# Eighteen of 24 gate tiles moved behind the first feed-forward stage, by seven products, and kept in HBM

## The chip, the cores and the metric

The kernel runs on one core of one Trainium2 chip. The metric is the device time of one execution in microseconds (us), shown as the median of the runs. One execution was also recorded by the hardware profiler; its span runs from the first to the last instruction.

## The reference, cut to what matters

Two layers of an encoder are applied to 656 tokens at once: 16 meta tokens and 512 prompt tokens (positions 0 to 527), and 8 streams of 16 sample tokens. Each layer is a feed-forward stage, a mixer and a second feed-forward stage. The gate logits that this change is about are 3 x 1024 of the 5376 columns of one projection; they scale the three branches of the mixer.

```python
h = x + 0.5 * swiglu(rmsnorm(x, n1), f1g, f1u, f1d)
u = rmsnorm(h, nm)
proj = u @ w_in
a_in, xb, gb, gc, q, k, v, g_logits = jnp.split(proj, cuts, axis=-1)
...
g = jax.nn.sigmoid(g_logits).reshape(bsz, t, N_BRANCH, D_MODEL)
mixed = g[:, :, 0] * y_a + g[:, :, 1] * y_b + g[:, :, 2] * y_c
h = h + mixed @ w_out
h = h + 0.5 * swiglu(rmsnorm(h, n2), f2g, f2u, f2d)
```

The inner sizes are D_MODEL 1024 and D_FF 2816, all in float32.

## The kernel before

Tokens lie along the free dimension and features along the 128 partitions, so the state `H` is 8 tiles of 128 x 656. Every float32 factor is split into a high and a low part (`split`: ScalarE (ACT) copies, VectorE (DVE) subtracts), and a product takes three matmuls (`mm3`, L145). A weight column tile of 1024 x 128 is loaded by SP into a `raw` buffer and split into two "slabs" (`prep_next`).

The work is one list of units, in order: first feed-forward stage, mixer, second feed-forward stage, for each of two layers (`build`, L1306). `run_units` takes them one after the other, and `pump` loads and splits the weights of the units that follow. A planner at build time then orders the instructions of each engine by simulated times, so neighbouring units interleave on TensorE (PE).

**A plain unit** (`unit`, `run_halves`, `col_unit`) is one column tile: 8 row tiles x 3 matmuls x 2 halves of the tokens = 48 matmuls. **A pair unit** (`pair_unit`, `run_pair`, L707) makes two column tiles by a seven-product scheme: x is kept as four blocks (two halves of the rows by two halves of the tokens) and four sums of them, and the seven products of 4 row tiles each take 7 x 4 x 3 = 84 matmuls of 328 columns where two plain units take 96. Its results come out over PSUM copies (ACT) and additions (DVE), and its weight sums are made by DVE or by accumulating DMAs that POOL issues (`grow`, L416). The feed-forward stages are made of pair units except for the first two column tiles of each matrix; the mixer is made of plain units alone.

**What feeds a stage.** The last units of a stage (`hu_down`) add to `H` and call `feed` (L526). For a feed-forward stage this writes the blocks of x with the old scale `rstd` in them and their four sums (`blocks`, `combine`), and the products are multiplied by `factor` = new scale x `root` of the old one. For the mixer it writes x times the gain alone, half by half (`gained`), and the products are multiplied by `rstd`. The new scale needs a sum over all 8 tiles and a chain of ACT and DVE steps (`scales`, `scale_of`).

**The mixer** (`mixer_units`, L1154) is 20 units for keys, queries, values, pool and conv, then 6 units for the gate tiles j = 0 and 1 (three branches each); attention jobs run beside them. After `done_gates` come 8 y units (`hu_y`, L1141), each with the three gate units of tile j + 2 behind it while there are any; then 8 w_out units. A y unit multiplies three PSUM results by the three gates, adds them and splits the sum, for each half of the tokens. In the second layer the gates and the y units leave the meta tokens out: their halves have 320 columns, not 328 (`EQ_OUT`). Gate tiles of even j lie in `gate[0]`, of odd j in `gate1`.

**Buffers.** The feed-forward stages have 8 slabs and 4 raw buffers, the mixer 4 and 2. PSUM has 2 banks named mm, 4 named z and 2 named aux. SP issues the weight loads in order; POOL issues the accumulating DMAs.

Of the kernel before, what the change touches and what calls it, by code (L numbers as in the profile page):

```python
# [10 lines left out]
P = 128  # L11
# [45 lines left out]
class Builder:  # L57
    def __init__(self, nc, tc, pools, t):
        self.nc, self.tc, self.t = nc, tc, t
        self.sb, self.wp, self.rp, self.pp = pools  # L60
# [95 lines left out]
    def setup(self):  # L156
# [17 lines left out]
        self.X = self.XR[:, 0:10496].rearrange("p (s k c) -> p s k c", s=2, k=KD)  # L174
        self.Pm = self.XR[:, 10496:15744].rearrange("p (s k c) -> p s k c", s=2, k=4)
        self.O = self.XR[:, 15744:20992].rearrange("p (s k c) -> p s k c", s=2, k=4)
# [8 lines left out]
        self.gate = [W[:, 0:1968], None]  # L185
# [340 lines left out]
    def feed(self, to, l, m, hi):  # L526

        c0, c1 = self.halves[hi]
        gain = {"mixer": "mix_norm", "ffn1": "ffn1_norm", "ffn2": "ffn2_norm"}[to]
        if to == "mixer":  # L530
            self.gained(self.H[:, m, c0:c1], l, m, c0, c1, gain)
        if hi == 0:
            return
        c0 = self.halves[0][0]
        n = c1 - c0
        if to != "mixer":
            self.blocks(l, m, gain, c0, n // 2)
        acc, s = self.acc[:, :n], self.sq[self.fed % 2][:, :n]
        if self.fed == 0:
            self.act(acc, self.H[:, m, c0:c1], AF.Square)  # L540
        else:
            self.act(s, self.H[:, m, c0:c1], AF.Square)
            if self.fed == KD - 1:
                self.tt(acc, acc, s, ALU.add)
            else:
                self.grow(acc, s)
        self.fed += 1
        if self.fed == KD:
            self.fed = 0
            halves = self.halves  # L550
            self.pending = lambda: self.scales(to, halves)
# [33 lines left out]
    def gained(self, h, l, m, c0, c1, gain):  # L585

        g = self.col(gain, l, m)
        hi, lo = (self.X[:, s, m, c0:c1] for s in range(2))
        return (self.act(hi, h, AF.Identity, scale=g),
                self.stt(lo, h, g, hi.bitcast(F32), ALU.mult, ALU.subtract))  # L590

    def scales(self, to, halves):

        at = halves[0][0]
        for c0, c1 in halves:
            n = c1 - c0
            ps = self.psum("aux")[:, :n]
            self.mm(ps, self.ones, self.acc[:, c0 - at:c1 - at], True, True)
            self.scale_of(ps, c0, c1, to != "mixer", self.na_f, self.nb_f)
# [41 lines left out]
    def col_unit(self, w, f, r, run):  # L641

        return dict(slabs=[4, 4], src=[(KD, [(0, KD, w[:, (f + r) * P:(f + r + 1) * P])])], prep=self.prep_plain,
                    run=self.run_col, evict=run, ring="F", r=r, i=0)
# [24 lines left out]
    def half_col(self, u, hi):  # L669
# [4 lines left out]
        S = self.sil if u["evict"] == self.gate_out else self.up  # L674
# [32 lines left out]
    def run_pair(self, u):  # L707
# [6 lines left out]
        S = self.sil if u["evict"] == self.gate_out else self.up  # L714
        S = S[:, :4 * n]
# [36 lines left out]

    def seven(self, u, bank, q, n, start):
# [19 lines left out]
    def x_at(self, s, k, c0, c1):  # L773
        return self.X[:, s, k, c0:c1]
# [35 lines left out]
    def scaled(self, out, ps, c0, c1):  # L810
        self.mul(out, ps, self.rstd[:, c0:c1])
# [25 lines left out]
    def hu_a(self, u, hi):  # L837
# [11 lines left out]
        else:  # L849
            n = TP - c0  # L850
            self.scaled(xp[:, PSTATE + c0:], ps[:, :n], c0, TP)
            self.mul(xs[:, :, PSTATE:], self.sample(ps[:, n:]), self.sample(self.rstd[:, TP:T]))
# [85 lines left out]
    def hu_gc(self, u, hi):  # L938
# [7 lines left out]
        else:  # L946
# [5 lines left out]
            self.mul(o, self.sample(ps[:, n:]), self.sample(self.rstd[:, TP:T]))  # L952
# [161 lines left out]

    def gate_unit(self, l, j, c):
        return self.w_in_unit(l, COL_G + 8 * c + j, self.hu_gate_logit, j=j, c=c)

    def hu_gate_logit(self, u, hi):
        ps, c0, c1 = self.w_in_product(u, hi)
        g = self.gate_of(u["j"])[:, 656 * u["c"] + c0:656 * u["c"] + c1]  # L1120
        self.scaled(g, ps, c0, c1)
        if u["j"] > 1:
            self.act(g, g, AF.Sigmoid)

    def gate_of(self, j):
        return self.gate1 if j % 2 else self.gate[0]
# [14 lines left out]
    def hu_y(self, u, hi):  # L1141
# [12 lines left out]
    def mixer_units(self, l):  # L1154
# [19 lines left out]
        def done_gates():  # L1174
# [131 lines left out]
    def build(self):  # L1306
# [23 lines left out]
        self.flush()  # L1330

# [231 lines left out]
def build_kernel(nc, tc, t):  # L1563
    from contextlib import ExitStack
    with ExitStack() as es:
# [5 lines left out]
        Builder(nc, tc, (sb, wp, rp, pp), t).build()  # L1571
# [42 lines left out]
```

## Time and profile before

| | |
|---|---|
| device time, median of 3 runs | 2848.79 us (2844.69 to 2854.1) |
| the profiled execution: device time | 2850.67 us |
| the profiled execution: span | 2849.0 us |
| PE busy | 2818.7 us, 99% |
| DVE busy | 1864.9 us, 65% |
| ACT busy | 1320.9 us, 46% |
| matmuls | 19179 |
| mean granted TensorE clock | 0.996 |

The time outside the span is 1.67 us. An engine's busy share is over the whole span; stages differ, so the rows below are taken by stage. A row of the timeline ends with the idle time of its engine before it and what ended that, in brackets.

### The profile page before, as it was taken

How to read it: one execution, taken by the hardware profiler on the slowest of the kernel's cores; microseconds unless marked ns; L12 is line 12 of the kernel's file. 1: busy time of each engine (PE TensorE's matmuls, PEld its weight loads, DVE VectorE, ACT ScalarE, POOL GpSimd, SP SyncE). 2: the span in 40 equal slices, each digit the busy share in tenths (PEclk: the TensorE clock that was granted, in tenths of full speed). 3: DMA queues.
4: the chain of work that ended last, by engine and by line, in shares of the span. 5: the costliest groups of instructions: out<-in, count | busy, mean ns of one | idle time of the engine just before them, and what ended most of it. 6: DMA issues, size and time to landing. Idle time of an engine off the chain costs nothing.

```text
span 2849.0 us, 48187 instructions
## 1 busy us (share of the span) xinstructions
PE 2818.7 (99%) x19179; PEld 2778.8 (98%) x19179; DVE 1864.9 (65%) x3442; ACT 1320.9 (46%) x2540; POOL 208.3 (7%) x305
## 2 busy tenths in 40 slices
PE   7999999999999999999999999999999999999999
PEld 6999999999999999999999999999999999999999
DVE  7675665876454776575786665768764457675764
ACT  5353444776332444353553443557763234443443
POOL 0001000011000001000000010001110000000010
PEclk8999999999999999999999999999999999999999
DMA  3545444222222345454435454442222224444452
GB/s 111 129 122 124 119 111 104 78 79 71 60 75 75 94 109 137 108 128 115 115 91 133 122 127 103 111 104 81 71 68 67 77 78 120 108 122 117 126 124 73
DMA packets 500244, 290.96 MB, mean 102 GB/s; under 512 B 14046, under 2 KB 477090, under 8 KB 500018
## 3 DMA queue, kind: packets, MB, share of 16 engines
q1 hardware_dynamic: 474468, 239.78, 29.2%
q0 software_dynamic: 25056, 47.79, 9.7%
q8 instruction: 150, 2.46, 0.4%
q14 instruction: 76, 0.62, 0.1%
q10 hardware_dynamic: 494, 0.32, 0.0%
HBM read 231.74 MB, written 8.31 MB: 84 GB/s over the span
## 4 chain that ended last, share of the span: by engine, by line
PE 94%; DVE 4%; DMA 2%; ACT 0%; issue 0%; SPq 0%; ACTq 0%; DVEq 0%
PE z L143 57%; PE mm L143 35%; DVE Wa L131 1%; PE aux L143 1%; DVE XR L134 1%; DVE ws L134 0%; DVE Wa L134 0%; DMA raw<-in_ffn_w_up_dram 0%; DMA raw<-in_ffn_w_gate_dram 0%; DVE slabs L134 0%; DMA xtok<-in_x_prompt_dram 0%; PE aux L1097 0%; PE z L1257 0%; DMA rawb<-rawb 0%; PE aux L1077 0%
## 5 line engine op out<-in xcount | busy, mean ns | idle before, releaser
L143 PE MATMUL mm<-XR,ws 128*128 128x328 f32 (+3 forms) x4848 | 799.3, 314 | 1.8 <-DVE Wa L134 1.8
L143 PEld LDWEIGHTS mm<-XR,ws 128*128 128x128 f32 x4848 | 737.1, 188 | 6.3 <-issue 2.9
L143 PE MATMUL z<-XR,ws 128*128 128x328 f32 (+3 forms) x3924 | 629.7, 312 | 10.0 <-ACT XR L120 5.9
L143 PEld LDWEIGHTS z<-XR,ws 128*128 128x128 f32 x3924 | 596.3, 189 | 11.6 <-ACT XR L120 6.4
L143 PE MATMUL z<-ra,ws 128*128 128x328 f32 (+1 forms) x2688 | 421.0, 311 | 0.8 <-DVE H L131 0.8
L120 ACT ACTIVATE ws<-raw 128x512 fp32r<-128x512 f32 (+1 forms) x429 | 264.3, 618 | 332.9 <-PE z L143 203.9
L143 PEld LDWEIGHTS z<-ra,ws 128*128 128x128 f32 x2688 | 405.1, 188 | 1.1 <-DVE H L131 1.0
L134 DVE TENSOR_TENSOR ws<-raw,ws 128x512 fp32r<-128x512 f32 (+1 forms) x429 | 288.1, 673 | 179.6 <-ACT ws L120 178.3
L143 PE MATMUL z<-ra,slabs 128*128 128x328 f32 (+1 forms) x2112 | 330.0, 312 | 0.0
L143 PEld LDWEIGHTS z<-ra,slabs 128*128 128x128 f32 x2112 | 319.2, 188 | 0.1
L143 PE MATMUL mm<-XR,slabs 128*128 128x328 f32 (+1 forms) x1944 | 316.7, 312 | 1.0 <-ACT Wa L120 1.0
L143 PE MATMUL z<-XR,slabs 128*128 128x328 f32 (+1 forms) x1764 | 296.5, 314 | 4.7 <-DVE Wa L134 4.7
L143 PEld LDWEIGHTS mm<-XR,slabs 128*128 128x128 f32 x1944 | 296.4, 188 | 1.4 <-ACT Wa L120 1.3
L143 PEld LDWEIGHTS z<-XR,slabs 128*128 128x128 f32 x1764 | 273.5, 190 | 5.4 <-DVE Wa L134 5.3
L134 DVE TENSOR_TENSOR Wa<-Wa 128x328 f32<-128x328 f32 (+5 forms) x325 | 215.5, 668 | 34.5 <-ACT Wa L120 31.0
L131 DVE SCALAR_TENSOR_TENSOR H<-z,H 128x328 f32<-128x328 f32 (+1 forms) x288 | 140.9, 493 | 141.2 <-PE z L143 140.8
L120 ACT ACTIVATE Wa<-Wa 128x656 f32<-128x656 f32 (+7 forms) x232 | 136.9, 597 | 98.1 <-DVE Wa L134 94.1
L120 ACT ACTIVATE slabs<-raw 128x512 fp32r<-128x512 f32 (+1 forms) x183 | 109.4, 601 | 156.6 <-PE z L143 75.3
L120 ACT ACTIVATE ws<-rawb 128x512 fp32r<-128x512 f32 (+1 forms) x183 | 109.5, 601 | 148.7 <-PE z L143 91.3
L120 ACT ACTIVATE slabs<-rawb 128x512 fp32r<-128x512 f32 (+1 forms) x181 | 107.4, 599 | 141.8 <-PE z L143 101.0
L120 ACT ACTIVATE Wa<-mm 128x328 f32<-128x328 f32 (+1 forms) x240 | 105.4, 439 | 141.2 <-PE mm L143 140.3
L134 DVE TENSOR_TENSOR ws<-rawb,ws 128x512 fp32r<-128x512 f32 (+1 forms) x183 | 118.8, 653 | 61.8 <-ACT ws L120 60.8
(181 smaller groups left out, 2549.8 us busy)
## 6 DMA issues: line engine op xcount, KB each, us to landing
raw<-in_w_in_dram SPq DMA_DIRECT2D x88, 512.0 KB, 3.7
raw<-in_ffn_w_gate_dram SPq DMA_DIRECT2D x57, 512.0 KB, 3.7
rawb<-in_ffn_w_up_dram SPq DMA_DIRECT2D x55, 512.0 KB, 4.9
rawb<-in_ffn_w_down_dram SPq DMA_DIRECT2D x48, 384.0 KB, 3.4
raw<-in_ffn_w_down_dram SPq DMA_DIRECT2D x48, 384.0 KB, 3.4
raw<-in_ffn_w_up_dram SPq DMA_DIRECT2D x33, 512.0 KB, 4.4
rawb<-in_ffn_w_gate_dram SPq DMA_DIRECT2D x31, 512.0 KB, 3.6
Wa<-in_ffn_w_gate_dram SPq DMA_DIRECT2D x36, 256.0 KB
```

The lines of the kernel that those rows point to most:

```text
L120: i = self.nc.scalar.activation(out, in_, func, **kw).ins
L131: return self.nc.vector.scalar_tensor_tensor(out, in0, scalar, in1, op0=op0, op1=op1).ins
L134: self.nc.vector.tensor_tensor(out, in0, in1, op=op)
L143: self.nc.tensor.matmul(out, lhsT, rhs, start=start, stop=stop, skip_group_check=True)
```

## The change

For each layer, the 18 gate tiles j = 2 to 7 leave the mixer. They are computed right behind the first feed-forward stage: two as plain column units, sixteen as eight pair units, over all 656 tokens in both layers. Each result goes through the sigmoid on ACT, and ACT's DMA queue stores it (128 x 656) to a tile in HBM. In the y stage POOL's DMA queue reads the three tiles of a j back into one of four places (`gates[0..2]` and `gate1`): j = 2 and 3 after `done_gates`, j + 4 after y unit j. The mixer reads x from the four blocks that `feed` now always writes, so its products are scaled by `factor`, of which `enter` keeps a copy in `root`; `done_y` puts `root` back as 1/`rstd`. `Pm` and `O` take the place of the four sums. The y units but the last add and split both halves at once.

```diff
-        if to == "mixer":
-            self.gained(self.H[:, m, c0:c1], l, m, c0, c1, gain)
         if hi == 0:
             return
...
-        if to != "mixer":
-            self.blocks(l, m, gain, c0, n // 2)
+        self.blocks(l, m, gain, c0, n // 2)
...
     def scaled(self, out, ps, c0, c1):
-        self.mul(out, ps, self.rstd[:, c0:c1])
+        self.mul(out, ps, self.root[:, c0:c1])
...
+    def early_gates(self, l):
+        w = self.t["w_in"][l]
+        units = []
+        for j in range(2, KD, 2):
+            for c in range(3):
+                f = COL_G + 8 * c + j
+                if not units:
+                    units = [self.col_unit(w, f, r, self.early_gate, j=j, c=c) for r in range(2)]
+                else:
+                    units.append(self.pair_unit(w, f, self.early_gate, soon=len(units) == 2, j=j, c=c))
+        return units
+
+    def early_gate(self, u, r, n):
+        s = self.place(u)[:, 2 * n * r:2 * n * (r + 1)]
+        self.act(s, s, AF.Sigmoid)
+        self.nc.scalar.dma_start(self.kept[3 * (u["j"] + r - 2) + u["c"]], s)
+
+    def load_gate(self, j):
+        if j < KD:
+            at = 3 * (j - 2)
+            self.nc.gpsimd.dma_start(self.gate_of(j).rearrange("p (c t) -> p c t", c=3),
+                                     self.kept[at:at + 3].rearrange("c p t -> p c t"))
...
     def gate_of(self, j):
-        return self.gate1 if j % 2 else self.gate[0]
+        return (self.gates[0], self.gate1, self.gates[1], self.gates[2])[j % 4]
...
             self.mul(g[c], self.product(ps, u["w"], x, ks, xks, c0, c1), g[c])
+        if j < KD - 1:
+            if hi == 0:
+                return
+            c0 = self.halves[0][0]
+            g = [self.gate_of(j)[:, 656 * c + c0:656 * c + c1] for c in range(3)]
         self.tt(g[0], g[0], g[1], ALU.add)
...
+            for j in range(2, 4):
+                self.load_gate(j)
         U[-1]["after_it"] = done_gates
         for j in range(KD):
             U.append(self.y_unit(l, j))
-            if j + 2 < KD:
-                for c in range(3):
-                    U.append(self.gate_unit(l, j + 2, c))
+            U[-1]["after_it"] = lambda j=j: self.load_gate(j + 4)
         self.last_y = len(U) - 1
-        U[-1]["after_it"] = self.ffn_columns
+
+        def done_y():
+            self.ffn_columns()
+            self.nc.vector.reciprocal(self.root, self.rstd)
+        U[-1]["after_it"] = done_y
...
             units += self.ffn_units(l, 1, ("mixer", l))
+            g = self.early_gates(l)
+            g[0]["before"] = lambda l=l: self.new_gates(l)
+            units += g
 
             def enter(l=l):
+                self.late()
+                self.nc.vector.tensor_copy(self.root, self.factor)
```

`place` gives column units and every second pair unit the buffer `sil`, the others `up`.

## Rows read from the trace of the kernel before

**Rows 1.** The page's first part: busy time, share of the span, instructions.
```profile
PE 2818.7 (99%) x19179; PEld 2778.8 (98%) x19179; DVE 1864.9 (65%) x3442; ACT 1320.9 (46%) x2540; POOL 208.3 (7%) x305
```

**Rows 2.** Stretches: length, each engine's busy time (instructions), clock, DMA share, GB/s.
```profile
20.00:100.00 80.00, 69.53 (x440) 67.78 (x441) 71.97 (x144) 47.15 (x95) 1.87 (x2) 0.94 0.30 83
...
372.00:426.00 54.00, 54.00 (x362) 54.00 (x361) 42.14 (x71) 29.31 (x56) 4.61 (x6) 1.00 0.48 121
...
745.00:938.00 193.00, 193.00 (x1285) 193.00 (x1284) 96.19 (x182) 58.38 (x108) 0.00 (x0) 1.00 0.26 74
938.00:997.00 59.00, 59.00 (x395) 59.00 (x394) 42.55 (x67) 24.98 (x36) 5.24 (x6) 1.00 0.42 95
...
1443.00:1458.00 15.00, 15.00 (x99) 14.65 (x98) 14.56 (x25) 8.32 (x12) 0.00 (x0) 1.00 0.20 52
```

**Rows 3.** The chain that ended last, in order of time: start, us, what.
```profile
737.83 7.22 PE z L143 x48
...
2173.87 7.04 PE z L143 x48
```

**Rows 4.** PE's timeline: its waits of over 1 us from 100 us on.
```profile
1016.89 9.02 PE L143 MATMUL z<-XR,slabs 128*128 128x328 f32 x48 [1.87 <-DVE Wa L134]
...
1908.69 0.55 PE L1077 MATMUL aux<-ident,Wa 128*128 128x128 f32 x3 [1.07 <-DVE Wa L131]
...
1911.00 3.78 PE L143 MATMUL mm<-XR,ws 128*128 128x384 f32 x20 [1.77 <-DVE Wa L134]
...
2409.60 0.85 PE L143 MATMUL z<-XR,ws 128*128 128x320 f32 x4 [1.13 <-ACT XR L120]
2423.66 8.84 PE L143 MATMUL z<-XR,slabs 128*128 128x320 f32 x48 [2.87 <-DVE Wa L134]
```

**Rows 5.** Groups by line and shape: busy us, mean ns; then idle time before.
```profile
L134 DVE TENSOR_TENSOR ws<-raw,ws 128x512 fp32r<-128x512 f32 x405 | 278.3, 688 | 177.1 <-ACT ws L120 175.8
...
L120 ACT ACTIVATE ws<-raw 128x512 fp32r<-128x512 f32 x405 | 254.4, 629 | 317.3 <-PE z L143 195.4 <-PE mm L143 84.2 <-issue 8.7
...
L134 DVE TENSOR_TENSOR Wa<-Wa 128x656 f32<-128x656 f32 x130 | 108.8, 837 | 1.5
...
L120 ACT ACTIVATE Wa<-mm 128x328 f32<-128x328 f32 x180 | 79.2, 440 | 103.1 <-PE mm L143 102.4
L134 DVE TENSOR_TENSOR Wa<-z,Wa 128x328 f32<-128x328 f32 x160 | 78.8, 494 | 52.1 <-PE z L143 48.1 <-ACT Wa L120 1.8
...
L120 ACT ACTIVATE Wa<-Wa 128x656 f32<-128x656 f32 x66 | 49.2, 748 | 32.8 <-DVE Wa L134 29.8 <-DVE Wa L131 2.6
...
L418 POOL DMA_DIRECT2D raw<-raw x36 | 31.0, 862 | 119.0 <-DVE Wa L131 33.3 <-DVE H L131 20.7 <-DVE ws L134 19.4
...
L112 ACT ACT_TABLE_LOAD x12 | 15.4, 1283 | 1.0 <-PEq L1602 0.8
```

**Rows 6.** DMA: queues (packets, MB, share of 16 engines), then issues (KB, us to landing).
```profile
q1 hardware_dynamic: 474468, 239.78, 29.2%
q0 software_dynamic: 25056, 47.79, 9.7%
...
raw<-in_w_in_dram SPq DMA_DIRECT2D x88, 512.0 KB, 3.7
...
Wa<-Wa POOLq DMA_DIRECT2D x24, 328.0 KB, 4.1
...
raw<-in_pool_proj_dram SPq DMA_DIRECT2D x16, 128.0 KB, 2.2
```

**Rows 7.** Timeline, first layer: the last attention output, y unit 0, an issue on SP.
```profile
734.05 0.44 PE L143 MATMUL z<-val 128*64 128x128 f32 x4
...
753.01 1.07 PE L143 MATMUL mm<-XR,ws 128*128 128x328 f32 x6
...
760.97 0.37 SPq L333 DMA_DIRECT2D raw<-in_pool_proj_dram  x1
```

More of the change, by code (lines that the diff above doesn't have):

```diff
@@ L59, in __init__ @@
         self.nc, self.tc, self.t = nc, tc, t
-        self.sb, self.wp, self.rp, self.pp = pools
+        self.sb, self.wp, self.rp, self.pp, self.dp = pools
         self.halves = HALF_ALL
@@ L173, in setup @@
         self.XR = sb.tile([P, XR], F32R, tag="XR", name="XR")
-        self.X = self.XR[:, 0:10496].rearrange("p (s k c) -> p s k c", s=2, k=KD)
-        self.Pm = self.XR[:, 10496:15744].rearrange("p (s k c) -> p s k c", s=2, k=4)
-        self.O = self.XR[:, 15744:20992].rearrange("p (s k c) -> p s k c", s=2, k=4)
+        v = self.XR.rearrange("p (s k e c) -> p s k e c", s=2, k=4, e=4)
+        self.X = [v[:, :, :, e, :] for e in range(2)]
+        self.Pm, self.O = v[:, :, :, 2, :], v[:, :, :, 3, :]
         scale = sb.tile([P, 2 * T], F32, tag="scale", name="scale")
@@ L184, in setup @@
         self.nb = W[:, o + 4 * 384:o + 5 * 384]
-        self.gate = [W[:, 0:1968], None]
+        self.gates = [W[:, 1968 * i:1968 * (i + 1)] for i in range(3)]
         o += 1968
@@ L550, in feed @@
             halves = self.halves
-            self.pending = lambda: self.scales(to, halves)
+            self.pending = lambda: self.scales(halves)
     def part(self, j):
@@ L583, in xs, with scales @@
         return self.XR[:, o:o + blocks * n]
[L585 to L592, printed above, removed]
+    def scales(self, halves):
         at = halves[0][0]
@@ L598, in scales @@
             self.mm(ps, self.ones, self.acc[:, c0 - at:c1 - at], True, True)
-            self.scale_of(ps, c0, c1, to != "mixer", self.na_f, self.nb_f)
+            self.scale_of(ps, c0, c1, True, self.na_f, self.nb_f)
     def scale_of(self, ps, c0, c1, factor, a, b):
@@ L639, in pair_unit, with col_unit @@
                     a21=w[0:4 * P, c[1]].rearrange("(k p) c -> p k c", p=P), **kw)
-    def col_unit(self, w, f, r, run):
+    def col_unit(self, w, f, r, run, **kw):
         return dict(slabs=[4, 4], src=[(KD, [(0, KD, w[:, (f + r) * P:(f + r + 1) * P])])], prep=self.prep_plain,
-                    run=self.run_col, evict=run, ring="F", r=r, i=0)
+                    run=self.run_col, evict=run, ring="F", r=r, i=0, **kw)
     def run_col(self, u):
@@ L673, in half_col @@
         ps = self.product(self.psum("z"), u["w"], x, SLOTS, SLOTS, c0, c1)
-        S = self.sil if u["evict"] == self.gate_out else self.up
+        S = self.place(u)
         self.mul(S[:, (2 * r + hi) * n:(2 * r + hi + 1) * n], ps, self.factor[:, c0:c1])
@@ L713, in run_pair @@
         f = self.factor[:, c0:c0 + 2 * n]
-        S = self.sil if u["evict"] == self.gate_out else self.up
-        S = S[:, :4 * n]
+        S = self.place(u)[:, :4 * n]
         s = [S[:, i * n:(i + 1) * n] for i in range(4)]
@@ L751, in run_pair, with place @@
         self.slot_tail()
+    def place(self, u):
+        if u["evict"] == self.early_gate:
+            return self.up if u.get("turn") else self.sil
+        return self.up if u["evict"] == self.up_out else self.sil
     def seven(self, u, bank, q, n, start):
@@ L773, in x_at @@
     def x_at(self, s, k, c0, c1):
-        return self.X[:, s, k, c0:c1]
+        return self.X[k // 4][:, s, k % 4, c0:c1]
     def pm_at(self, s, k, c0, c1):
@@ L851, in hu_a @@
             self.scaled(xp[:, PSTATE + c0:], ps[:, :n], c0, TP)
[L852 removed]
+            self.mul(xs[:, :, PSTATE:], self.sample(ps[:, n:]), self.sample(self.root[:, TP:T]))
             assert self.history
@@ L951, in hu_gc @@
             o = xs[:, :, 2:]
-            self.mul(o, self.sample(ps[:, n:]), self.sample(self.rstd[:, TP:T]))
+            self.mul(o, self.sample(ps[:, n:]), self.sample(self.root[:, TP:T]))
             self.mul(o, o, self.sample(self.cB[:, TP:T]))
@@ L1330, in build, with new_gates @@
         self.flush()
+    def new_gates(self, l):
+        self.kept = self.dp.tile([3 * (KD - 2), P, T], F32, tag=f"gates{l}", name=f"gates{l}")
     def load_consts(self):
@@ L1570, in build_kernel @@
               for tag, n in (("mm", 2), ("z", 4), ("aux", 2))}
-        Builder(nc, tc, (sb, wp, rp, pp), t).build()
+        dp = es.enter_context(tc.tile_pool(name="dram", bufs=1, space=bass.MemoryType.DRAM))
+        Builder(nc, tc, (sb, wp, rp, pp, dp), t).build()
 _INS = ["x_prompt", "x_sample", "cache_k", "cache_v", "state_pool", "state_conv", "meta", "ffn1_norm",
```

5 lines of the change are left out of this document (1 added, 4 removed).

## The prediction, made before the changed kernel was run

> **What bounds the kernel now.** I read the busy shares first: PE is at work for 2818.7 of 2849.0 us [rows 1]. So the time is the number of matmuls times what one takes, plus about 30 us in which PE stands; a change pays by matmuls it drops, and costs where it makes PE stand. Second, the stretches: in the y stage, from 745 to 938 us, PE works 193.00 of 193.00 us, with DVE at 96.19 and ACT at 58.38 [rows 2]. Nothing there but the matmul count can be shortened. Third, the chain: 48 matmuls of 328 columns take 7.22 us, 48 of 320 columns 7.04 us [rows 3], so 150.4 and 146.7 ns each. Last, PE's waits: behind the first 100 us five exceed 1 us, all at the opening of a stage, 8.7 us together [rows 4].
>
> **1. The matmuls.** Before, a layer's 18 gate tiles take 18 x 48 = 864 matmuls. After, two column units take 96 and eight pair units 8 x 84 = 672, together 768. First layer: 96 fewer at 150.4 ns, 14.4 us. Second layer: 864 at 146.7 ns (126.7 us) become 768 at 150.4 ns (115.5 us), because the early tiles are made for all 656 tokens; that leaves 11.2 us. Sum: **-25.6 us**. All of it is on the path, as PE has no idle time where the tiles stood or where they go. Matmuls must number 19179 - 192 = 18987.
>
> **2. What the pair units ask of the other engines.** A pair lasts 84 x 150.4 ns = 12.6 us. DVE: 7 slab subtractions at 688 ns, 2 weight sums of that size, 5 results of 328 columns at 494 ns, one product of 656 at 837 ns [rows 5]: 9.5 us. ACT: 7 slab copies at 629 ns, 3 PSUM copies at 440 ns, 2 sigmoids at 748 ns [rows 5] make 7.2 us, and two stores are issued. An issue on ACT's queue has no good row; SP's takes 0.37 us [rows 7], POOL's 0.86 us [rows 5], so 0.7 to 1.7 us a pair. Feed-forward pairs carry as much: from 372 to 426 us DVE is busy 42.14, ACT 29.31 of 54 us and PE never stands [rows 2]. The store must wait for its sigmoid, and behind it on ACT queue the next PSUM copy and slab copies; PE needs that copy before it adds the fourth product to the same bank, two products or 3.6 us later. A wait of about one sigmoid (0.75 us) and one issue fits in. I take 0; without that slack each of 36 stores would cost up to 1 us.
>
> DMA: those 54 us use 0.48 of the engines [rows 2]. The stores add 2 x 328 KB per pair; at the hardware queue's own rate (239.78 MB in 29.2% of 2849 us, 288 GB/s [rows 6]) 2.3 us of 12.6, so 0.66 in all. POOL gets two issues of 0.86 us per pair [rows 5]; SP gets 14 loads of 256 KB more (0.37 us of issue each), and the gate weights only change their place on its queue. I take 0.
>
> **3. The opening of the early gates.** The first products need the new scale before their PSUM banks come free, as at every feed-forward stage. Two such openings have PE waits: 1.87 us at 1016.89, and 1.13 + 2.87 us about 2409 to 2424 [rows 4]; the third, from 1443 to 1458 us, has none, with DVE at 14.56 of 15 us [rows 2]. Here weights can be loaded ahead as in the third, but the first pair comes after four half units instead of eight, so its sums compete for DVE. Between 0 and 4 us a layer; I take 1.5, nearer the third: **+3.0 us**. Writing the blocks of x for the mixer is hidden as it is under w_out, where PE works 59.00 of 59.00 us with DVE at 42.55 [rows 2].
>
> **4. The entry of the mixer.** Its first keys and queries no longer wait for a new scale, which is old by then. In the second layer PE waits 1.07 + 1.77 us there for these results [rows 4]: **-2.8 us**. New is the change from 8 slabs and 4 raw buffers to 4 and 2 right behind pairs instead of w_down units. If the first key weights came late PE would wait one load, 3.7 us [rows 6], per layer; the last pair gives 12.6 us to hide it. I take 0, with 0 to 7.4 kept for the range.
>
> **5. The y stage.** 26 units become 8, in a row: 57.8 us. DVE per y unit of 7.22 us: 6 products of 494 ns, 2 additions and a subtraction of 656 columns at 837 ns, 2 slabs at 688 ns [rows 5]: 6.85 us, against about 3.7 us per unit before (96.19 us over 26). ACT has 2 us. So DVE goes from half to 95% by these durations, and somewhat less on its queue, as neighbours overlap. Six PSUM banks hold a whole unit, which smooths it. Gains I exclude, as PE has no idle time there; the loss lies between 0 and the 13% that PE loses where DVE is that full, from 20 to 100 us (PE 69.53 of 80, DVE 71.97 [rows 2]): 15 us over 16 units. That stretch is also the program's start, with weights that arrive late; the opening at 1443 us ran DVE at 97% and lost nothing. I take 1 us a layer: **+2.0 us**. The reciprocal at the stage's end is off the path: w_out's first results can wait in four banks, four half units long.
>
> The way back of the gates: POOL's `load_gate` waits for DVE's products of y unit j, and behind it stand only the next `load_gate` and w_out's accumulations; a product of y unit j + 4 on DVE waits for it, with slab work queued behind. Six blocks of 984 KB a layer. Loads of 128 and 512 KB land in 2.2 and 3.7 us [rows 6], which extended gives 5.5 us for one. The first two can start after the last attention read at 734 us, y unit 2 comes 14 us behind the 753 us at which y unit 0 begins [rows 7], and each later block has three units, 21.7 us. I take 0.
>
> That DMAs of all queues share one set of engines speaks against this. A unit's weights take 0.26 of 7.22 us [rows 2], 1.9 us; a block at the software queue's rate (47.79 MB in 9.7% of 2849 us, 173 GB/s [rows 6]) 5.8 us: together 7.7 us, half a microsecond over the unit. The Trainium skill ("DMA: Bandwidth & Descriptors", Issuing engines are not separate DMA queues) says the same: transfers from scalar, sync and gpsimd interleave on the same 16 engines, so another queue saves issue time alone. By that rule the sum would lose 0.5 us x 6 x 2 = 6 us if the blocks had no lead; the row's lead of three units takes that up.
>
> ACT loads a function table more often, twice a layer at 1.28 us [rows 5], both with slack on ACT.
>
> **Sum.** -25.6 + 3.0 - 2.8 + 2.0 = -23.4 us on the profiled execution's 2850.67 us gives 2827.3. That execution stands 1.9 us above the median of the runs, so **2825 us**, against 2848.79: -0.8%. About 0.3% (8.5 us) is what a measurement of this kernel can tell from no change: faster is below 2840.2, slower above 2857.3.
>
> **The rivals.** *A: the y stage is paced by DVE.* For it: 6.85 of 7.22 us, in order, with slab work between the products. Against: the full stretch at 1443 us. At 13% of 115 us it costs 15 us instead of my 2: 2838 us, and with an opening that stands as long as the worst one in rows 4 in both layers, +5 us, 2843 us: no change.
>
> *B: the gates come back too slowly, and the kernel is slower.* A product that waits for its block holds DVE's queue, then the slabs, then PE. Six blocks pass one after the other; y unit 7 needs the last about 50.5 us after y unit 0 begins. With r us per block the loss is 6r - 50.5 a layer: none up to 8.4 us, and the whole gain is gone at r = 10.4. For it: a 328 KB accumulation takes 4.1 us to land [rows 6], three of them 12.3 us, which costs 2 x 23.3 = 47 us: 2872 us. Against: that DMA reads two operands, and part of its 4.1 us is fixed; the plain loads give 5.5 us.
>
> *C: the openings go well.* If the early gates open like the stage at 1443 us, and the planner's new order also removes the waits at 1016 and 2409 to 2424 us [rows 4], the sum is -25.6 - 2.8 - 5.9: 2815 us. Against: those weights arrive late by the rule that holds them until the y units are done, which stays.
>
> That the change does not do what it says can hardly be; the matmul count shows it.
>
> **How the numbers follow.** My forecast, 2818 to 2834 us, has 0.70; A 0.15, half of it still below 2840.2; B 0.07; C 0.08. Faster: 0.70 + 0.08 + 0.07 = 0.85. Same: the rest of A, 0.08. Slower: B, 0.07. The range reaches from C, 2815, to A with its long openings, 2843; what it leaves out is B and the edges.
>
> **What would show it.** In the changed profile: 18987 matmuls at the same 150 ns; the y stage in 58 us with PE full; the entry of the second mixer without a wait of over 1 us; the opening of the early gates with 0 to 4 us. DVE near 95% with PE waiting for it in the y stage shows A. DVE waiting for DMA on the gates there shows B. Wrong would be everything if pair matmuls behind the feed-forward stage ran at another spacing, or if ACT's stores held up PSUM copies in each pair.

## The result, and the profile after

The changed kernel takes **2818.59 us** (median of 3 runs, 2816.9 to 2819.91) against 2848.79 before: a ratio of 0.9892, 95% interval 0.9865 to 0.992. That is 30.2 us less; 23.8 were forecast (2825 us). Its profiled execution took 2816.9 us, with a span of 2815.2.

First the page of the kernel after: busy shares and DMA queues [rows 1, 6]. Matmuls number 18987, as counted; PE still works 99% of the span, so the program is as much bound by matmuls as before. Queue q10 (ACT's) grows from 0.32 to 12.41 MB by the 36 stores, and q0 (POOL's) carries 19.4 MB more: 12 blocks of gates on their way back, 12.1 MB, and the weight sums of 14 pair units.

```profile
PE 2787.8 (99%) x18987; PEld 2750.0 (98%) x18987; DVE 1970.0 (70%) x3564; ACT 1374.2 (49%) x2598; POOL 242.5 (9%) x345
...
q1 hardware_dynamic: 481860, 243.45, 29.9%
q0 software_dynamic: 31584, 67.22, 12.6%
q10 hardware_dynamic: 5678, 12.41, 1.2%
```

Its DMA issues (KB each, median us from issue to landing), the two that are new. Ten of the twelve blocks go to `Wa`, the row shown; two go to `Wb`, and over all twelve the landing takes 5.2 to 8.1 us, 5.6 at the median:

```profile
gates<-Wa ACTq DMA_DIRECT2D x36, 328.0 KB, 3.0
...
Wa<-gates POOLq DMA_DIRECT2D x10, 984.0 KB, 5.6
```

Its stretches [rows 2]: the block of early gates, the y stage, and the seven microseconds of the y stage in which most data moves. PE stands in none of them.

```profile
475.00:592.00 117.00, 117.00 (x775) 116.66 (x774) 85.29 (x146) 64.87 (x115) 13.30 (x16) 1.00 0.61 167
867.00:924.00 57.00, 57.00 (x380) 57.00 (x379) 51.89 (x88) 16.67 (x26) 3.06 (x4) 1.00 0.48 145
888.00:895.00 7.00, 7.00 (x49) 7.00 (x48) 6.17 (x12) 2.02 (x3) 0.76 (x1) 1.00 0.87 259
```

PE's waits of over half a microsecond behind the first 100 us are these four [rows 4]. None lies in the early gates, at the mixer's entry (before: 1.07 + 1.77 us) or in the y stage. All are at the openings of the second feed-forward stages, which the change leaves alone.

```profile
988.74 0.88 PE L143 MATMUL z<-XR,ws 128*128 128x328 f32 x4 [0.76 <-ACT XR L120]
...
1002.46 7.48 PE L143 MATMUL z<-XR,slabs 128*128 128x328 f32 x48 [2.15 <-DVE Wa L134]
...
2378.06 0.86 PE L143 MATMUL z<-XR,ws 128*128 128x320 f32 x4 [0.90 <-ACT XR L120]
...
2392.12 7.31 PE L143 MATMUL z<-XR,slabs 128*128 128x320 f32 x48 [2.87 <-DVE Wa L134]
```

Cut by the starts of PE's matmuls in the two profiled executions, the 33.8 us between the spans lie here (the part ahead of the first row is 0.1 us longer after):

| stretch | before | after | difference | forecast |
|---|---|---|---|---|
| first layer, gates and mixer to w_out | 464.78 | 448.92 | -15.86 | -11.9 |
| second feed-forward, next first one | 944.25 | 944.39 | +0.14 | 0 |
| second layer, gates and mixer to w_out | 462.11 | 446.40 | -15.71 | -11.5 |
| w_out and the rest | 502.8 | 500.3 | -2.5 | 0 |

### The profile page after: what moved, and what is told of

The parts are those of the page before. It is cut to its first block, busy times and chain, and to the rows that moved or that the text cites. A ratio compares the mean times of both kernels' runs of the same rounds, so it can differ in the third digit from the quotient of the medians.

```text
span 2815.2 us, 48237 instructions
## 1 busy us (share of the span) xinstructions
PE 2787.8 (99%) x18987; PEld 2750.0 (98%) x18987; DVE 1970.0 (70%) x3564; ACT 1374.2 (49%) x2598; POOL 242.5 (9%) x345
## 3 DMA queue, kind: packets, MB, share of 16 engines
q10 hardware_dynamic: 5678, 12.41, 1.2%
## 4 chain that ended last, share of the span: by engine, by line
PE 95%; DVE 3%; DMA 1%; issue 0%; ACT 0%; SPq 0%; ACTq 0%
PE z L143 56%; PE mm L143 37%; PE aux L143 1%; DVE XR L134 1%; DVE Wa L131 1%; DVE Wa L134 0%; DVE ws L134 0%; DMA raw<-in_ffn_w_gate_dram 0%; DMA raw<-in_ffn_w_up_dram 0%; DVE slabs L134 0%; DMA xtok<-in_x_prompt_dram 0%; PE aux L1091 0%; PE z L1281 0%; PE aux L1071 0%; DVE rawb L134 0%
## 5 line engine op out<-in xcount | busy, mean ns | idle before, releaser
L143 PE MATMUL z<-XR,ws 128*128 128x328 f32 (+3 forms) x3132 | 515.5, 313 | 10.5 <-ACT XR L120 6.4
L143 PEld LDWEIGHTS z<-XR,ws 128*128 128x128 f32 x3132 | 480.0, 189 | 12.5 <-ACT XR L120 7.2
L143 PE MATMUL mm<-XR,slabs 128*128 128x328 f32 (+1 forms) x2328 | 379.9, 312 | 0.9 <-ACT Wa L120 0.9
L143 PE MATMUL z<-XR,slabs 128*128 128x328 f32 (+1 forms) x2172 | 361.3, 312 | 5.0 <-DVE Wa L134 5.0
L143 PEld LDWEIGHTS mm<-XR,slabs 128*128 128x128 f32 x2328 | 355.3, 188 | 1.3 <-ACT Wa L120 1.2
L143 PEld LDWEIGHTS z<-XR,slabs 128*128 128x128 f32 x2172 | 333.2, 188 | 6.0 <-DVE Wa L134 5.5
L134 DVE TENSOR_TENSOR ws<-raw,ws 128x512 fp32r<-128x512 f32 (+1 forms) x382 | 255.6, 672 | 108.6 <-ACT ws L120 106.5
L134 DVE TENSOR_TENSOR Wa<-Wa 128x328 f32<-128x328 f32 (+6 forms) x369 | 249.2, 680 | 60.8 <-ACT Wa L120 56.4
L134 DVE TENSOR_TENSOR Wa<-z,Wa 128x328 f32<-128x328 f32 (+1 forms) x280 | 136.7, 492 | 73.6 <-PE z L143 64.9
L134 DVE TENSOR_TENSOR slabs<-raw,slabs 128x512 fp32r<-128x512 f32 (+1 forms) x212 | 138.6, 656 | 59.6 <-ACT slabs L120 58.5
```

The source lines that it names most:

```text
L134: self.nc.vector.tensor_tensor(out, in0, in1, op=op)
L143: self.nc.tensor.matmul(out, lhsT, rhs, start=start, stop=stop, skip_group_check=True)
```

## The experiments

The times stand against 2818.59 us for the changed kernel. Each run's ratio is to the kernel before, measured beside it on the same chip. There that kernel took 2848.2 to 2849.2 us. The intervals are 0.1 to 0.2% to each side, so differences of two or three us between runs are not told apart by time alone. The edits are cut to what matters.

### 1. Is it the matmuls? (plain_tiles)

```diff
-                if not units:
-                    units = [self.col_unit(w, f, r, self.early_gate, j=j, c=c) for r in range(2)]
-                else:
-                    units.append(self.pair_unit(w, f, self.early_gate, soon=len(units) == 2, j=j, c=c))
+                alt = len(units) // 2 % 2
+                units += [self.col_unit(w, f, r, self.early_gate, j=j, c=c, alt=alt) for r in range(2)]
```

(`place` goes by `alt`, and `enter` no longer finishes a last pair, as there is none.)

> The changed kernel with its 18 early gate tiles all as plain column units: 864 matmuls a layer instead of 768, 19179 in all as before. The tiles still lie behind the first feed-forward stage, go to HBM and come back, and the mixer still reads the four blocks. Theory M (the gain is the matmuls that the pair units save, plus small waits that go): 2 x 96 matmuls at 150.4 ns come back, 28.9 us on 2818.6, so 2844 to 2851 us, likeliest 2847.5. Rival P (the gain is the place: no wait at the mixer's entry, a smoother mixer, a clean y stage; the pair units' own load on DVE and ACT eats part of what they save): at most half of that comes back, 2819 to 2833 us.

Measured: 2845.8 us, ratio 0.9989 (0.9979 to 0.9998). 27.2 of the forecast 28.9 us came back, far outside the range of P. The page's first row has the old count of matmuls:

```profile
PE 2819.9 (99%) x19179; PEld 2783.2 (98%) x19179; DVE 1897.4 (67%) x3448; ACT 1316.7 (46%) x2486; POOL 218.0 (8%) x317
```

In the first layer, the 868 matmuls from the start of the early block (864 and four for the scale's sum) last 131.25 us here, and the 772 (768 and four) 116.86 in the changed kernel: 14.39 us for 96 matmuls, 150 ns each, so the pair units cost nothing beyond their matmuls. (In the changed kernel 13 of the 772 are already wider ones of the mixer, about 0.3 us, as the planner mixes the two at the border.) The place, the store, the way back and the calmer entry are together worth the 3.4 us (by the interval 0.6 to 6) that this kernel lies below the one before, with the 3.2 us already paid that the second layer's wider tiles cost (864 x 3.7 ns).

### 2. How full may DVE be in the y stage? (adds_by_halves, two_more_adds, six_more_adds)

```diff
-        if j < KD - 1:
-            if hi == 0:
-                return
-            c0 = self.halves[0][0]
-            g = [self.gate_of(j)[:, 656 * c + c0:656 * c + c1] for c in range(3)]
```

> The changed kernel with the additions and the split of each y unit done half by half again. Per y unit DVE gets six operations of 328 columns at 494 ns in place of three of 656 at 837 ns, 0.45 us more: 3.2 us a layer, so about 55 us of the y stage's 57 where the changed kernel has 51.89. Theory S (the stage has slack: six PSUM banks smooth it, DVE delays nobody up to its full share): 2818 to 2821 us, PE full in the stage. Rival A (DVE paces the stage already and each of its microseconds shows): 2 x 3.2 us, 2824 to 2827 us, with PE waits on DVE in the stage.

```diff
             g = [self.gate_of(j)[:, 656 * c + c0:656 * c + c1] for c in range(3)]
+            for i in range(2):
+                self.tt(g[i], g[i], g[i], ALU.max)
```

> The changed kernel with two more DVE operations of 656 columns in each of the first seven y units of a layer (the maximum of a buffer with itself, which leaves the values as they are): 7 x 2 x 0.84 = 11.8 us a layer where DVE has 57.0 - 51.89 = 5.1 us free. Theory S: 6.7 us a layer are too many; a part of it slides into the next stage, where four banks cover up to 14 us: 0 to 6.7 us a layer, 2819 to 2832 us, likeliest 2824, with PE waits on DVE late in the stage. Rival A: all of it shows, 2 x 11.8 us, 2840 to 2844 us.

Measured: 2817.69 us (0.9894, 0.9879 to 0.9908) and 2818.5 us (0.99, 0.9885 to 0.9915). Neither costs anything, and for the second my likeliest 2824 was too high. Its y stage, by the same cut as above, shows DVE busy for 56.21 of 57.00 us and PE without a gap:

```profile
867.00:924.00 57.00, 57.00 (x380) 57.00 (x379) 56.21 (x98) 14.25 (x23) 3.05 (x4) 1.00 0.47 145
```

Its DVE rows (start, duration) say why. The next operation starts before the one ahead of it has ended: 0.60 us from the start of a 512-column operation to the next, 0.41 for 328, 0.75 for 656, where the durations are 0.69, 0.49 and 0.83. A sum of durations overstates what a stretch asks of the engine. The Trainium skill ("Vector Engine (DVE) Microarchitecture Reference", Measured stream behaviour on trn2) gives operations with one or two sources, measured there on 32-bit integers, 1.04 ns a column plus about 75 ns after queue overlap; worked out, that estimate is 0.61, 0.42 and 0.76 us, and the trace agrees.

```profile
910.47 0.69 DVE L134 TENSOR_TENSOR ws<-raw,ws 128x512 fp32r<-128x512 f32 x1
911.07 0.49 DVE L134 TENSOR_TENSOR Wa<-z,Wa 128x328 f32<-128x328 f32 x1
911.48 0.83 DVE L134 TENSOR_TENSOR Wb<-Wb 128x656 f32<-128x656 f32 x1
912.23 0.49 DVE L134 TENSOR_TENSOR Wa<-mm,Wa 128x328 f32<-128x328 f32 x1
912.64 0.83 DVE L134 TENSOR_TENSOR Wa<-Wa 128x656 f32<-128x656 f32 x1
```

So a third dose, with six operations in place of the two:

> The changed kernel with six more DVE operations of 656 columns in each of the first seven y units (values unchanged), where two more cost nothing. Theory Q (DVE's capacity goes by the spacing of its starts, which in the run with two more were 0.41 us for 328 columns, 0.60 for 512, 0.75 for 656, not by their durations of 0.49, 0.69, 0.84): a y unit needs 6 x 0.41 + 3 x 0.75 + 2 x 0.60 = 5.9 us, with six more 10.4 us of 7.22, 22 us a layer too many. What slides into the next stage is covered by up to 14 us: 8 to 22 us a layer, 2835 to 2863 us, likeliest 2847, with PE waiting for DVE in the stage. Rival D (capacity goes by the durations): 11.9 us a unit, 33 us a layer too many, 2857 to 2884 us. Rival Z (these operations hide elsewhere, whatever their number): 2817 to 2822 us.

Measured: 2851.91 us (1.0014, 1.0004 to 1.0023), 33 us more: in Q's range and 5 above its likeliest, below D's. From y unit 0 to w_out's first matmul the stages last 13.0 and 15.1 us longer. PE's waits on DVE, two in each layer:

```profile
905.40 2.01 PE L143 MATMUL z<-XR,ws 128*128 128x328 f32 x6 [6.43 <-DVE Wa L134]
...
917.61 2.01 PE L143 MATMUL z<-XR,ws 128*128 128x328 f32 x6 [2.49 <-DVE Wb L134]
...
2315.54 1.97 PE L143 MATMUL mm<-XR,ws 128*128 128x320 f32 x6 [6.76 <-DVE Wa L134]
...
2328.09 1.97 PE L143 MATMUL mm<-XR,ws 128*128 128x320 f32 x6 [3.23 <-DVE Wb L134]
```

The waits are 8.9 and 10.0 us. The rest of the 13.0 and 15.1 goes with the clock: behind a wait the granted clock is below 1.00, so a part of the matmuls ran at 1.2 instead of 2.4 GHz (rows of the first layer; behind POOL's busy time come the clock, the DMA share and GB/s). What is left of the 33 us lies in w_out, where PE waits for the late sums, 1.61 + 1.49 us in the first layer and 1.37 in the second.

```profile
890.00:905.00 15.00, 8.97 (x60) 8.70 (x58) 15.00 (x24) 3.27 (x5) 0.77 (x1) 0.95 0.43 137
905.00:918.00 13.00, 10.11 (x49) 9.84 (x50) 13.00 (x22) 2.77 (x4) 1.52 (x2) 0.76 0.47 136
918.00:945.00 27.00, 25.39 (x160) 25.11 (x159) 27.00 (x47) 5.67 (x9) 0.77 (x1) 0.95 0.39 125
```

### 3. What do the gates on their way back cost? (two_places, one_place, loads_twice)

```diff
-        return (self.gates[0], self.gate1, self.gates[1], self.gates[2])[j % 4]
+        return (self.gates[0], self.gate1)[j % 2]
...
-            for j in range(2, 4):
-                self.load_gate(j)
...
-            U[-1]["after_it"] = lambda j=j: self.load_gate(j + 4)
+            U[-1]["after_it"] = lambda j=j: self.load_gate(j + 2)
```

> The changed kernel with two places for the gates in the y stage instead of four: block j + 2 is loaded into the place of y unit j, so its lead is one unit, 7.2 us, not three. The order of work is otherwise the same. My theory L (a block takes POOL 0.8 us to issue and lands 5.3 us behind the issue's start at the median, 8.1 at most): just enough, 0 to 4 us, 2817 to 2823 us. Rival B (a block takes 8 us or more from the last use of its place to its first use): three reloads of each place one after the other, 2 to 10 us a layer, 2823 to 2839 us.

Measured: 2818.66 us (0.9895, 0.988 to 0.991), as L said. A lead of one unit is just enough. One PE wait in the y stage of each layer shows that it is no more than that; the first layer's:

```profile
886.32 1.17 PE L143 MATMUL z<-XR,ws 128*128 128x328 f32 x6 [0.72 <-DVE Wa L134]
```

```diff
-        return (self.gates[0], self.gate1, self.gates[1], self.gates[2])[j % 4]
+        return (self.gates[0], self.gate1, self.gates[1])[min(j, 2)]
...
-            U[-1]["after_it"] = lambda j=j: self.load_gate(j + 4)
+            U[-1]["after_it"] = lambda j=j: self.load_gate(j + 1 if j > 1 else KD)
```

(`done_gates` loads block 2 alone.)

> The changed kernel with one place for all gates from j = 2 on: block j + 1 is loaded only when y unit j is done on DVE, so five blocks a layer have no lead at all. Theory L: per such unit about 6.1 us from the last use to the landing, and DVE's own work of 5 to 6 us behind it, together 11 to 12 us where PE needs 7.22: 4 to 5 us late five times, less one unit that the six PSUM banks cover: 13 to 25 us a layer, 2845 to 2869 us, likeliest 2857. Rival B (10 us or more a block): 35 us a layer or more, above 2888 us. Rival H (a lead is hardly needed, the loads hide anyway): below 2830 us.

Measured: 2863.03 us (1.0053, 1.0038 to 1.0068), 44.4 us more: in L's range. The mechanism of rival B exists, then: without lead the change loses all it gains and more. In the first layer DVE's first product with a new block waits 0.60 to 0.97 us for the DMA each time, and PE waits for that product. The first such wait on DVE, the first layer's five on PE, and the stretch:

```profile
896.89 0.50 DVE L134 TENSOR_TENSOR Wa<-z,Wa 128x328 f32<-128x328 f32 x1 [0.97 <-DMA Wa<-gates]
```

```profile
897.44 1.26 PE L143 MATMUL z<-XR,ws 128*128 128x328 f32 x6 [2.97 <-DVE Wa L134]
...
909.09 2.01 PE L143 MATMUL z<-XR,ws 128*128 128x328 f32 x6 [2.60 <-DVE Wa L134]
...
920.75 1.15 PE L143 MATMUL z<-XR,ws 128*128 128x328 f32 x6 [2.83 <-DVE Wa L134]
...
932.50 2.01 PE L143 MATMUL z<-XR,ws 128*128 128x328 f32 x6 [2.72 <-DVE Wa L134]
...
944.30 2.97 PE L143 MATMUL z<-ra,ws 128*128 128x328 f32 x18 [2.79 <-DVE Wa L134]
```

```profile
867.00:958.00 91.00, 77.09 (x465) 75.75 (x465) 58.56 (x101) 20.32 (x31) 3.86 (x5) 0.92 0.37 114
```

Each of the five blocks makes PE stand for 2.6 to 3.0 us, 13.9 together, but this y stage lasts 78.97 us instead of 57.97. The other 7.1 us fit the clock, 0.92 over these 91 us: a wait that comes back every 12 us costs here half as much again as it shows.

```diff
-            self.nc.gpsimd.dma_start(self.gate_of(j).rearrange("p (c t) -> p c t", c=3),
-                                     self.kept[at:at + 3].rearrange("c p t -> p c t"))
+            for _ in range(2):
+                self.nc.gpsimd.dma_start(self.gate_of(j).rearrange("p (c t) -> p c t", c=3),
+                                         self.kept[at:at + 3].rearrange("c p t -> p c t"))
```

> The changed kernel with every block of gates loaded twice into its place. Theory L (a load of 984 KB takes 5.6 us, two of them 11.2; the first two blocks start 27 us ahead of y unit 0, the others three units ahead): block 7 lands about when y unit 7 begins, so 0 to 3 us, 2817 to 2822 us. Rival B (the transfers share the engines with 1.9 us of weights a unit and go one behind the other, six blocks in the way worked out in the prediction: 6 x 11.2 - 50.5 us a layer): 33 us, 2852 us.

Measured: 2817.6 us (0.9893, 0.9878 to 0.9907), as L said. Its y stage, and the busiest seven microseconds of it:

```profile
875.00:925.00 50.00, 50.00 (x333) 50.00 (x332) 44.25 (x80) 14.86 (x23) 6.11 (x8) 1.00 0.71 234
882.00:889.00 7.00, 7.00 (x49) 7.00 (x48) 6.11 (x11) 2.76 (x4) 1.53 (x2) 1.00 0.97 320
```

The DMA engines are at 0.97 and 320 GB/s there: the two loads into one place follow each other, but those into neighbouring places overlap. The lead is now used up to the last: one product in the first layer's y stage waited for its block.

```profile
910.35 0.50 DVE L134 TENSOR_TENSOR Wa<-z,Wa 128x328 f32<-128x328 f32 x1 [0.91 <-DMA Wa<-gates]
```

### 4. Do the stores hold up ACT? (stores_twice)

```diff
-        self.nc.scalar.dma_start(self.kept[3 * (u["j"] + r - 2) + u["c"]], s)
+        for _ in range(2):
+            self.nc.scalar.dma_start(self.kept[3 * (u["j"] + r - 2) + u["c"]], s)
```

> The changed kernel with every gate tile stored twice, so 36 more issues of 0.33 us on ACT's queue (11.8 us) and 11.8 MB more traffic beside the pair units. My theory (ACT has slack there, 64.87 us busy of 117): no change, 2817 to 2821 us. Rival K (PSUM copies and slab copies behind the issues come late and PE with them): a third or more of the 11.8 us, 2822 to 2831 us, with PE waits on ACT between 490 and 592 us.

Measured: 2818.33 us (0.9894, 0.9881 to 0.9908), no change. The block of early gates, with the DMA share at 0.73 instead of 0.61:

```profile
475.00:592.00 117.00, 117.00 (x774) 116.66 (x773) 84.14 (x145) 64.27 (x114) 11.76 (x15) 1.00 0.73 211
```

### 5. What do the two column units at the opening do? (first_pair)

```diff
-                if not units:
-                    units = [self.col_unit(w, f, r, self.early_gate, j=j, c=c) for r in range(2)]
-                else:
-                    units.append(self.pair_unit(w, f, self.early_gate, soon=len(units) == 2, j=j, c=c))
+                units.append(self.pair_unit(w, f, self.early_gate, soon=len(units) < 2, j=j, c=c))
...
     def new_gates(self, l):
+        while self.todo:
+            self.todo.pop(0)()
```

(`finish_pending` also moves up in `run_pair`, right behind the first product. With an odd number of pairs, `enter` also advances `clock` by one where it is even, so that attention's jobs keep their turns; the versions of experiments 6 and 7 have that line too.)

> The changed kernel whose first two early tiles are a pair unit as well (nine pairs), so the sums of x that the two column units had covered are made by DVE and ACT ahead of it, and the scale's chain follows the pair's first product: 2 x 12 matmuls fewer, 18963, 3.6 us. Theory O (the opening's cost is only hidden by the two column units): four results of 328 columns and two splits of 1312 on DVE (about 7 us) stand between the last w_down unit and the pair's third product, 3.6 us behind its start: PE waits 3 to 8 us a layer, 2821 to 2831 us, likeliest 2825. Rival C (openings cost nothing): 2815 us.

Measured: 2826.21 us (0.9926, 0.9913 to 0.9938), as O said. The first layer's opening, and four of PE's waits in it, on the sums of x (XR) and on slabs:

```profile
475.00:505.00 30.00, 23.25 (x134) 19.98 (x133) 26.69 (x47) 16.74 (x28) 3.31 (x5) 1.00 0.43 107
```

```profile
485.21 2.22 PE L143 MATMUL z<-XR,slabs 128*128 128x328 f32 x13 [1.10 <-DVE slabs L134]
...
488.67 0.57 PE L143 MATMUL z<-XR,slabs 128*128 128x328 f32 x2 [1.10 <-DVE XR L134]
...
492.76 0.42 PE L143 MATMUL z<-XR,slabs 128*128 128x328 f32 x1 [1.47 <-ACT XR L120]
...
494.32 0.57 PE L143 MATMUL z<-XR,slabs 128*128 128x328 f32 x2 [0.84 <-DVE XR L134]
```

24 matmuls fewer and still 7.6 us more: by the medians the two early blocks lose 11.2 us that the column units had covered. In the two profiled executions the first 760 matmuls of a block (nine pairs and the scale's sum) take 124.63 and 121.23 us where the changed kernel's first 760 take 115.04 and 115.01, 9.6 and 6.2 us; this execution was 2.9 us shorter ahead of the first block, which the change does not touch. PE stands for 6.75 us of the 30 in the row above, within O's 3 to 8; the rest of the 9.6 lies in slower matmuls between the waits.

### 6. How far does the step carry? (twenty_early, twentytwo_early)

```diff
-        for j in range(2, KD, 2):
-            for c in range(3):
+        for j in range(0, KD, 2):
+            for c in range(3) if j else EARLY:
...
+            for j in range(2):
+                for c in EARLY:
+                    self.nc.gpsimd.dma_start(self.gate_of(j)[:, 656 * c:656 * (c + 1)], self.kept[3 * j + c])
```

`EARLY` names the branches of j = 0 and 1 that are made early too: (2,) gives twenty early tiles, (1, 2) twenty-two. Their plain units and sigmoids in the mixer fall away.

> The changed kernel with the two tiles of the third branch for j = 0 and 1 moved as well: nine pair units instead of eight, and two plain units of 48 matmuls less in the mixer: 24 matmuls fewer in all, 18963. First layer 12 x 150.4 ns = 1.8 us, second 96 x 146.7 - 84 x 150.4 ns = 1.4 us. Theory T (behind the last attention product, at 851.8 us of the changed kernel, two plain gate units still run before y unit 0; so two can go and attention keeps its cover): 2815.3 us, 2813 to 2817. Rival: the last attention output, through DVE and ACT, is then needed at once by y unit 0, and PE waits 2 to 5 us a layer: 2819 to 2826 us.

Measured: **2813.14 us** (0.9874, 0.9859 to 0.9889), faster than both kernels, 5.5 us below the changed one where 3.3 were expected. Its runs took 2810.35 to 2813.88 us; those of adds_by_halves, which runs like the changed kernel and was measured beside it, 2815.9 to 2821.61. So the gain is clear, but whether it is 3.3 or 5.5 us is not. As T said, y unit 0 (from 863.22 us) follows on the last attention products without a wait; only eight matmuls of the last gate unit stand between:

```profile
860.93 1.06 PE L146 MATMUL z<-val,Wa 128*64 128x16 f32 x32
861.92 1.46 PE L146 MATMUL mm<-XR,ws 128*128 128x328 f32 x8
863.22 1.96 PE L146 MATMUL z<-XR,ws 128*128 128x328 f32 x12
```

The entry of the second feed-forward stages also lost its waits of 0.76 and 0.90 us in this trace. That is 1.7 us, so the rest is within the noise.

> Two pairs instead of one on top of the eighteen tiles (the second and third branch of j = 0 and 1): ten pair units, only two plain gate units left in the mixer, 18939 matmuls, 6.5 us of matmuls less than in the changed kernel. Theory T (with twenty tiles y unit 0 starts right behind the last attention product, so nothing that covers attention is left to move): the last four attention steps lose two units of cover, and PE waits for DVE and ACT there, 5 to 14 us a layer: 2822 to 2841 us, likeliest 2830. Rival: attention's chain is shorter than its cover and only the matmuls count: 2811 us.

Measured: 2825.61 us (0.9924, 0.9909 to 0.9939), 12.5 us slower than with twenty: T's mechanism. Attention's last two steps stand bare, in the first layer:

```profile
864.01 1.22 PE L146 MATMUL z<-att,ntri 128*128 128x512 f32 x2 [3.09 <-DVE att L137]
...
867.56 0.70 PE L146 MATMUL z<-val 128*64 128x128 f32 x4 [1.90 <-POOL val L1563]
```

```profile
845.00:895.00 50.00, 45.01 (x312) 43.03 (x312) 30.71 (x50) 20.24 (x35) 5.73 (x10) 0.90 0.40 126
```

The second layer's trace has 1.18 and 1.90 us at the same places, 8.1 us in all. The clock takes about as much again: 0.90 over these 50 us, 0.94 over the 60 us of the second layer up to 2275 us. A small part of the first wait is not attention's own. POOL issued a block's load right ahead of attention's masks:

```profile
860.69 0.77 POOL L1133 DMA_DIRECT2D Wa<-gates  x1 [14.44 <-ACT XR L123]
861.47 0.52 POOL L1561 TENSOR_SCALAR_AFFINE_SELECT val<-val 128x256 f32<-128x256 f32 x1
```

What the masks read was ready at 860.74 us, so up to 0.7 of the 3.09 us stem from the load's place in POOL's queue. The wait of 1.90 us does not: POOL had stood idle for 3.85 us before the masks that end it.

### 7. The opening that is left (twenty_early_not_soon)

```diff
-                soon = ci == 0
+                soon = ci == 0 and which == 1
```

> The version with twenty early tiles, and besides, in the second feed-forward stage of each layer, the weight sums of the first pair units made by accumulating DMAs as those of all later pairs, instead of by DVE (four operations of 0.69 us per pair of units less in the opening). Theory W (that opening's PE wait, 2.15 and 2.87 us, with the slower clock that can follow it, is DVE work queued ahead of the results): the waits shrink by 1 to 2 us each, 2808 to 2812 us, likeliest 2810.5. Rival V (the sums come late through DMA, and PE waits for the slabs of the first pairs): 2814 to 2830 us. Rival N (DVE is not what decides there): 2812.5 to 2814 us.

Measured: 2812.6 us (0.9881, 0.9867 to 0.9895): no difference from twenty early tiles that these runs can tell. That is in N's range, but the upper end of W's, 2812, is too near to be told from it by time. What speaks against W is that the waits did not both shrink. They changed places: the first layer's grew from 2.25 to 3.39 us, the second layer's of 3.02 went, and 1.49 us came up ahead of it. What decides in that opening stays open.

```profile
1001.67 7.93 PE L146 MATMUL z<-XR,slabs 128*128 128x328 f32 x51 [3.39 <-DVE Wa L137]
```

## Why the prediction was right

**Matmuls (-25.6 forecast).** Right, and most of the gain: 18987 of them, 116.86 and 116.80 us for the first 772 matmuls of the two early blocks where 772 x 150.4 ns make 116.1, and 27.2 us lost again in plain_tiles. (The projection has 256 + 768 + 1536 + 3072 = 5632 columns, not 5376; the 24 gate tiles are as counted.)

**The pair units' load (0).** Right. DVE took 85.29, ACT 64.87 of 117 us, PE 117. A store's issue took 0.33 us on ACT, below my lower bound of 0.37, and 36 more of them changed nothing. ACT's sum had left out one of four PSUM copies of a pair, 0.44 us, so it is 7.7 and not 7.2 us; the slack was wide enough for that. The DMA share was 0.61 where 0.66 was forecast.

**The opening of the early gates (+3.0).** Too high: 0. PE has no wait there in either layer. I took a value between two kinds of opening; the one at 1443 us [rows 2] was the right model. That this is because the early units' weights are loaded ahead in the same way was argued and not tried. That the cover is real, and not that openings are free, is shown by first_pair.

**The entry of the mixer (-2.8).** Right: both waits of [rows 4] are gone, and the change of rings cost nothing. Besides, what is left of a layer's mixer got 1.4 us shorter in the first layer and 1.65 in the second than these terms say. The comparison of the two traces spreads this over attention's small products, whose starts follow a little closer; PE's idle time in the first layer's mixer is only 0.2 us before and 0 after. The cause stays open.

**The y stage (+2.0).** Too high: 0. It lasts 57.97 us against 57.8 forecast, with PE full. The step that failed is the sum of DVE durations, 6.85 of 7.22 us per unit: by the spacing of starts a unit needs 5.9, and 1.3 us are free, so two more operations of 0.75 us overran by 0.2. The reciprocal's 4.25 us come on top in the same stage: 8 x 5.9 + 4.25 = 51.5 us, near the 52 us that DVE is busy. So with two more operations the stage asked for about 4 us more of DVE than it lasts, and PE did not show it. I had said "somewhat less on its queue, as neighbours overlap", and then priced the stage by the full sum. Rival A fell: at the dose that adds 1.5 us per unit there was no loss, at 4.5 us there was.

**The way back of the gates (0).** Right, with the lead of three units as its reason: one unit suffices barely, none costs 44 us. A block lands in 5.6 us, the estimate was 5.5. Rival B's sum of blocks one after the other was too strict. The first two are issued 27 and 15 us ahead of y unit 0 (the rows below), and neighbouring loads overlap, so doubled loads were hidden where that sum gave 33 us.

POOL's queue after, first layer (in brackets, what ended the wait before each issue):

```profile
839.52 0.81 POOL L1130 DMA_DIRECT2D Wa<-gates  x1 [1.02 <-ACT XR L120]
...
850.68 0.80 POOL L1130 DMA_DIRECT2D Wa<-gates  x1 [4.51 <-PE z L143]
882.34 0.77 POOL L1130 DMA_DIRECT2D Wa<-gates  x1 [30.86 <-DVE Wb L134]
...
900.58 0.77 POOL L1130 DMA_DIRECT2D Wa<-gates  x1 [6.49 <-DVE Wa L134]
```

That transfers share the engines shows in the shares (0.87, and 0.97 with doubled loads) and in the landing, 6.5 us at the median with doubled loads instead of 5.6. Those are loads of one queue, POOL's. Between queues the traces show less: of SP's loads of 256 KB for a y unit (attn_proj) eight recorded ones landed in 2.8 to 3.6 us before, the two recorded ones after in 3.0 and 7.0. The Trainium skill ("DMA: Bandwidth & Descriptors", Issuing engines are not separate DMA queues) says that DMAs of all issuing engines interleave on the same 16 engines, and the trace agrees as far as it goes. The 6 us worked out by it did not show, since the lead covers them.

One sentence of that part was incomplete: behind `load_gate` on POOL there also stand attention's mask operations. In the changed kernel nothing waited for it; with twenty-two early tiles it held the masks up by as much as 0.7 us.

**Table loads (0).** Right: 16 instead of 12, at 1.283 us, hidden. The reciprocal, which I let run at the end of the y stage, ran at its beginning for 4.25 us:

```profile
L112 ACT ACT_TABLE_LOAD x16 | 20.5, 1283 | 1.1 <-PEq L1635 0.8
...
L1209 DVE RECIPROCAL scale<-scale 128x656 f32<-128x656 f32 x2 | 8.5, 4254 | 0.1
```

**The sum** was -23.4 us, measured -33.8 between the profiled executions and -30.2 between the medians. Of the 10.4 us between forecast and profile, 5.0 are the two terms that turned out 0 and 3.1 the mixer's small products. About 2.5 lie in the last stretch of the table, where the change does nothing. There the 48 matmuls behind the 2.87 us wait took 7.31 us after and 8.84 before [rows 4], and a wait of 0.79 us at 2487 us is missing. The same wait was followed by 8.84 us in adds_by_halves and 8.85 in stores_twice, and by 8.65 or more wherever else a row shows these 48 matmuls, so that this profiled execution had 7.31 is a matter of the execution; the medians, nearer by 3.6 us, fit that. Rival C was half right: the early openings went well, but the waits at the second feed-forward stages stayed. By time alone it did better than the forecast: 2818.59 lies 0.6 us inside the lower end of 2818 to 2834 and nearer to C's 2815 than to 2825. So the mechanism was right, but three sizes (the two openings, the y stage, the mixer's small products) erred to the same side, and the time came out at the edge of the forecast.

## What to carry to other kernels

Where PE has no gaps, price a change by its matmul count and then ask of every moved piece what covers it: what the pair units save came to the count within two microseconds (27.2 of 28.9 us), and each cover that an experiment took away cost more than could be won by it: a block's lead 44 us, the column units at the openings 11 us for 3.6 us of matmuls, the last plain units beside attention 12.5 us net. Read an engine's room from the spacing of its starts in a stretch where it runs back to back, not from the sum of its durations. And go on with a step that pays until its cover runs out: two tiles more were worth 3 to 5 us, four cost 7.

## What the hardware showed unexpectedly

- **DVE's operations overlap**: 0.75, 0.60 and 0.41 us from start to start where 0.83, 0.69 and 0.49 us are shown as durations (656, 512 and 328 columns). DVE busy at 56.21 of 57 us held nobody up.
- **A reciprocal is dear**: 4.25 us for 128 x 656, five times an addition of that size (0.84 us).
- **A wait costs more than itself**: behind PE waits of 2 to 3 us, 48 matmuls took 7.3 to 7.5 us with the clock at 1.00, or 8.7 to 10.1 with a granted clock below 1.00, thus some at 1.2 GHz. Which of the two follows differs between runs with the same wait: 2.15 us was followed by 7.48 us after, and by 8.99 in stores_twice (row below). Waits that come back every 12 us lowered the clock to 0.92 for the whole stretch.

```profile
1001.36 8.99 PE L143 MATMUL z<-XR,slabs 128*128 128x328 f32 x48 [2.15 <-DVE Wa L134]
```
